# Heads on sixteen even places of each slot, and M0 and N0 made a slot earlier

## The chip, the cores and the metric

The kernel runs on one core of one Trainium2 chip. The metric is the device time in microseconds. A core has five engines that run side by side and are tied together by semaphores: TensorE (PE in the profile; PEld is its loading of weights), VectorE (DVE), ScalarE (ACT), GpSimd (POOL) and SyncE (SP), which here issues all transfers between HBM and the on-chip memory. Products land in PSUM, which has banks of 512 floats per partition.

## The reference

A two-layer encoder does one inference step for 512 prompt frames and eight groups of 16 sample frames: 640 rows of 1024 features. What matters here is branch B of a layer, the gated delta rule with eight heads:

```
h = rmsnorm(x, ln1); proj = h @ w_in                      # all branches at once
q, k, v = silu(causal_conv(qkv)) per head; q, k l2-normed # 128 features a head
for each head:   S_t = a_t (I - b_t k_t k_t^T) S_{t-1} + b_t k_t v_t^T ;  o_t = S_t^T q_t
o = rmsnorm(o, o_norm) * silu(z)
x += (sigmoid(gA) * (zA @ p_a) + sigmoid(gB) * (zB @ p_b)) @ w_o
x += relu(rmsnorm(x, ln2) @ w_up)^2 @ w_down
```

The recurrence is computed in exact block form: a unit lower triangular system over a block of frames is solved, and then a short chain runs over the blocks. Branch A is a gated MLP with a spatial product over 128 frames.

## The kernel before

Activations lie feature by row: 128 partitions of features, 640 rows. A weight block is 128 by 1024; it is loaded by SP (`raw`, three buffers), split by ScalarE and VectorE into a high and a low part (`whi`, `wlo`, lines 133 and 134), and multiplied in three products (high-high, high-low, low-high). One block is 16 units of `gemm` (line 196), a unit being three matmuls of 320 columns.

The order of TensorE's instructions is the program's own: it is scheduled by hand (line 1115). The other engines' orders are worked out when the program is built, from priorities: an instruction counts as so many places earlier as the offset of `tc.high_priority` says. `AHEAD` is 200; the chain below has twice that, the roots 1.

In the phase `heads` of a layer the blocks of q, k, v and of the gates are taken in ten slots of 4, 7, 5, 5, 5, 5, 5, 5, 5 and 6 blocks (line 792). Beside the gemm of slot h three pieces of work for three different heads are laid between its units, each a generator that yields how far ahead its next hop is:

- `prepare` of head h-1: transposes of K (`kt`, line 508) into the two banks of tag "d", squares and the copy `kg` out of them (lines 510 to 512), Gram products (`gp`, three hops) with their masked copies into `AP_` (line 527), transposes of V (`vt`), then the recurrence X on VectorE for the blocks of 16 (lines 577 to 583), the decays E of the next head on ScalarE (line 487), and two hops that join the blocks to 32: `Y3` and `Z3` (lines 601 and 605).
- `chain` of head h-2: makes the masked operands M0 and N0 (lines 624 to 630), joins blocks to 64 and 128 in the hops Y, M1/Z, Y2 and N2, and then runs the chain over four blocks of 128 frames with the hops w, S/o and kS; the sample frames run beside it (`sample`, line 675). Its banks have tag "c", the sample's tag "d".
- `roots` of head h-3: squares of the output, means over 128 features by a product with ones (`ms`, line 767, two halves, tag "d"), a row to HBM (line 777), back as columns, the power -1/2 on GpSimd, and back to HBM (line 784).

Tags "c" and "d" have two banks each, and a product that takes a bank waits until what the bank held has been read. In slot 0 the preparation's place is taken by `gating`: the products for beta and the decay rates, their transposes, a long chain of small VectorE operations (lines 380 to 406), the cumulative sums and a row that goes through HBM. In slot 9 there is no preparation, and the chain of the last head is followed by its roots.

How the hops come to their units is decided in `paced`. Before, each work has a length of its own (`CHAIN` 66, `PREPARE` 70, `ROOTS` 26, `GATING` 48, and the slot's own number of units for roots); a hop that is due at d of length L comes at unit d n / L of n, rounded up. In a slot of five blocks (80 units) that gives these units:

| work | units of its hops |
|---|---|
| chain | 0 (M0, N0), 10 (Y), 15 (M1/Z), 21 (Y2), 26 (N2), 31 (w), 36, 40, 45, 50, 55, 60, 65, 70, 74, 79 |
| prepare | 0 (kt), 13, 18, 22 (gp), 27 (vt), 31, then X from 36 to 68, 76 (Y3), 80 (Z3, behind the slot's last unit) |
| roots | 0, 8 and 18 (ms), 22 |

After the heads, `merge` runs the product for v of branch A (`va`, weights w_v) while `zb` (line 964) loads what the roots left and makes the operand of the next product.

Of the kernel before, what the change touches and what calls it, by code (L numbers as in the profile page):

```python
# [9 lines left out]
F32 = mybir.dt.float32  # L10
# [7 lines left out]
P = 128  # L18
# [4 lines left out]
H = 8  # L23
DEPTH = 2
EPS = 1e-6
NB = 8
# [11 lines left out]

CHAIN, PREPARE, ROOTS, GATING = 66, 70, 26, 48
AHEAD = 200  # L40
# [22 lines left out]
def encoder(ctx, tc, xin, wblk, wba, sct, sdelta, prow, pcol, gates, wst, bsr, convw, consts, delta0,  # L63
# [162 lines left out]

    def paced(work, n, ahead=AHEAD):


        length, gen = work  # L230
        due = 0
        for u in range(n):
            while due * n <= u * length:
                with tc.high_priority(offset=ahead):
                    due += next(gen, length)
            yield
        run(gen)

    def in_turn(first, second):
        yield from first  # L240
        yield 1
        yield from second()
# [116 lines left out]
    def gating(l, pk, pl, out):  # L359
# [4 lines left out]
        if l + 1 < DEPTH:  # L364
            nc.sync.dma_start(wb, wba[l + 1])
        yield 15

# [6 lines left out]
        nc.scalar.activation(v2(baT[0:32, :]), ps[0:32, :, 0:HT], AF.Copy)  # L374
        yield 4
        pt = bank("d", f"baT{l}")
# [30 lines left out]
        gf = g.rearrange("p t h -> p (t h)")  # L407
        yield 24
        pc = bank("d", f"cum{l}")
# [18 lines left out]
        nc.scalar.activation(dec[:, 4:12, :].rearrange("p t h -> p (t h)"), tot[:, 80:144], AF.Exp)  # L428
        yield 6
        pr = bank("d", f"row{l}")  # L430
# [6 lines left out]
        er = later(l, 0, pl, out["gate"])  # L437
        yield 8
        decays(l, 0, pl, out["gate"], er, out)
# [50 lines left out]
    def prepare(l, h, pl, act, gate, out):  # L490
# [24 lines left out]
        nc.vector.scalar_tensor_tensor(sn, sn, -1.0, beta[:, :, h], op0=ALU.mult, op1=ALU.mult)  # L515
        yield 11

        AP_ = pl.tile([P, 5, 2, P], F32, tag="AP", bufs=2, name=f"AP{nm}")
        for ts in ((0, 1), (2, 3), (4,)):
            b = bank("d", f"gp{nm}{ts[0]}")  # L520
            for t in ts:
                o = b[:, (t % 2) * 256:(t % 2) * 256 + 256]
                mm(o[:, 0:P], kT[:, t, :], kT[:, t, :], True, True)
                mm(o[:, P:256], kT[:, t, :], qT[:, t, :], True, True)
            for t in ts:
                o = b[:, (t % 2) * 256:(t % 2) * 256 + 256]
                nc.vector.scalar_tensor_tensor(AP_[:, t], o.rearrange("p (a n) -> p a n", a=2), sn[:, t:t + 1],
                                               rep(E[:, t, :], 1, 2), op0=ALU.mult, op1=ALU.mult)
            if t < 4:
                yield 4  # L530

# [15 lines left out]
        nc.gpsimd.tensor_tensor(qg[:], qT[:], er[:], op=ALU.mult)  # L547
        yield 4
        v0, v1 = tok(vT, f"vt{nm}")
# [3 lines left out]
        nc.vector.tensor_tensor(vn[:, 4:5, :], v1, rep(nk[:, 4:5], 2, P), op=ALU.mult)  # L553
        yield 4
        QT = pl.tile([P, 4, 64], F32, tag="QT", bufs=1, name=f"QT{nm}")
# [6 lines left out]
        if h + 1 < H:  # L562
            er = later(l, h + 1, pl, gate)
        yield 4

# [11 lines left out]
        for j in range(15):  # L577
            n = slice(j + 1, 16)
            nc.vector.tensor_tensor(pr[:, :, n], Bj[j], rep(X[:, :, j], 2, 15 - j), op=ALU.mult)
            if j + 2 < 15:  # L580
                row(j + 2)
            nc.vector.tensor_tensor(X[:, :, n], X[:, :, n], pr[:, :, n], op=ALU.add)
            yield 2
        if h + 1 < H:
# [6 lines left out]
        nc.vector.transpose(m16[:].rearrange("p t n -> p (t n)"), n0c[:, 0:4, :].rearrange("p t n -> p (t n)"))  # L591
        yield 5
        def joined(lhsT, rhs, nm2):
# [9 lines left out]
        nc.scalar.activation(y32[:], by, AF.Copy)  # L603
        yield 4
        bz = joined(y32, n0c, f"Z3{nm}")
        nc.vector.tensor_tensor(n0c[:, 0:4, :], n0c[:, 0:4, :], bz, op=ALU.add)
        sq = pl.tile([P, 5, P], F32, tag="sq", bufs=2, name=f"sq{nm}")
        nc.scalar.activation(sq[:], qT[:], AF.Square, scale=(P * EPS) ** 0.5)
        S8 = pl.tile([P, NB, P], F32, tag="S8", bufs=2, name=f"S8{nm}")
        nc.sync.dma_start(S8[:], sdelta[l, :, h].rearrange("b d e -> d b e"))  # L610
        out[h] = sq, kT, qg, kg, AP_, vn, n0c, QT, S8


    halves = (slice(0, 64), slice(64, 128))
    quarters = tuple(slice(32 * i, 32 * i + 32) for i in range(4))

    def chain(l, h, pl, gate, out):
        sq, kT, qg, kg, AP_, vn, n0c, QT, S8 = out.pop(h)
        beta, ngam, egam, dL, dec, rowd = gate
        kb, qb, N1 = kbs[h % 2], qbs[h % 2], n1s[h % 2]  # L620
        nm = f"{l}{h}"


# [4 lines left out]
        for dst, src, n in ((M0, m0c, 4), (N0, n0c, 5)):  # L628
            for b in range(2):
                nc.vector.tensor_scalar(dst[:, :, 32 * b:32 * b + 32], src[:, 0:n, :], odd[:, b:b + 1], None, op0=ALU.mult)  # L630
        yield 8
        by = bank("c", f"Y{nm}")
# [5 lines left out]
        nc.scalar.activation(Y[:], bys, AF.Copy)  # L638
        yield 4
        b1 = bank("c", f"M1{nm}")  # L640
# [9 lines left out]
        for hf in halves:  # L650
            nc.vector.tensor_tensor(N1[hf, :, hf], bzs[hf], N0[hf, 0:4, :], op=ALU.add)
        yield 5
# [4 lines left out]
        yield 4  # L657
# [4 lines left out]
        yield 4  # L662

# [51 lines left out]
        for t in range(4):  # L715
            if t:
                pk = bank("c", f"kS{nm}{t}")
                mm(pk[:, 0:P], kT[:, t, :], S[:], True, True)
                y = pl.tile([P, P], F32, tag="y", bufs=1, name=f"y{nm}{t}")
                nc.vector.scalar_tensor_tensor(y[:], pk[:, 0:P], egam[:, t, h:h + 1], vn[:, t, :], op0=ALU.mult, op1=ALU.add)  # L720
                if t >= 2:
                    next(beside)
                yield 4
# [5 lines left out]
            yield 4  # L729
# [12 lines left out]
            o_done(po, t)  # L742
            if t < 3:
                yield 4
        nc.sync.dma_start(dp_out[l, h], S[:])
# [3 lines left out]

    def roots(l, h, pl, ond, msd, out):  # L750
        osb, sq = out.pop((h, "o"))
# [19 lines left out]
        nc.sync.dma_start(ond[h], of)  # L771
        yield 8
        means(0, sh)
        sh = squares(1)
        yield 10
        means(1, sh)
        nc.sync.dma_start(msd[0][h:h + 1, :], so[0:1, :])
        yield 4

# [35 lines left out]
    def heads(l, ond, msd, gd, close, norm):  # L815
# [70 lines left out]
        with phase(f"heads{l}", 1) as pl:  # L886
# [15 lines left out]
            for h, slot in enumerate(heads_blocks()):  # L902

                n = 16 * len(slot)
                work = []
                if h == H + 1:
                    work.append(paced((CHAIN + ROOTS, in_turn(
                        chain(l, h - 2, pl, out["gate"], out), lambda: roots(l, h - 2, pl, ond, msd, out))), n, 2 * AHEAD))
                elif h >= 2:
                    work.append(paced((CHAIN, chain(l, h - 2, pl, out["gate"], out)), n, 2 * AHEAD))  # L910
                if h >= 3:
                    work.append(paced((n, roots(l, h - 3, pl, ond, msd, out)), n, 1))
                if 1 <= h <= H:
                    work.append(paced((PREPARE, prepare(l, h - 1, pl, act, out["gate"], out)), n))
                if h == 0:
                    work.append(paced((GATING, gating(l, pl, pl, out)), n))
# [303 lines left out]
```

## Time and profile before

| | |
|---|---|
| median of 3 runs | 2526.88 us (2524.76 to 2527.54) |
| the profiled execution | 2525.81 us, its span 2523.8 us |
| granted TensorE clock | 0.994 |
| busy: TensorE, VectorE, ScalarE, GpSimd | 98%, 52%, 40%, 23% of the span |
| slots 3, 4 and 5 of layer 0, one window each | 52.50, 52.75 and 52.75 us |

The span runs from the first to the last instruction of the profiled execution. A row of a timeline gives start, duration, engine, line, operation, tiles as out<-in, shapes and how often; in brackets stands how long the engine was idle before it and what released it. Matmuls overlap, so the price of one is read from the distance between starts, not from its duration. Products of 32-bit floats appear as two instructions.

### The profile page before, as it was taken

How to read it: one execution, taken by the hardware profiler on the slowest of the kernel's cores; microseconds unless marked ns; L12 is line 12 of the kernel's file. 1: busy time of each engine (PE TensorE's matmuls, PEld its weight loads, DVE VectorE, ACT ScalarE, POOL GpSimd, SP SyncE). 2: the span in 40 equal slices, each digit the busy share in tenths (PEclk: the TensorE clock that was granted, in tenths of full speed). 3: DMA queues.
4: the chain of work that ended last, by engine and by line, in shares of the span. 5: the costliest groups of instructions: out<-in, count | busy, mean ns of one | idle time of the engine just before them, and what ended most of it. 6: DMA issues, size and time to landing. Idle time of an engine off the chain costs nothing. (4 is left out here: it accounts for less than half of the span.)

```text
span 2523.8 us, 45089 instructions
## 1 busy us (share of the span) xinstructions
PE 2466.8 (98%) x18456; PEld 2386.9 (95%) x18456; DVE 1308.1 (52%) x2693; ACT 1020.7 (40%) x1958; POOL 585.5 (23%) x647
## 2 busy tenths in 40 slices
PE   7999999999999999999999999999999999999997
PEld 7999999998999999999999999999989999999997
DVE  7756677536555433333356677664285653333333
ACT  4666666633123212121347666774332222122122
POOL 3223333211222202011213333331112221011012
PEclk9999999999999999999999999999999999999998
DMA  4323323336532222222233333333465222222221
GB/s 153 101 98 114 113 95 95 111 125 240 161 107 68 76 76 76 75 75 74 78 102 110 106 95 95 100 112 114 150 225 150 91 68 76 76 76 76 76 69 65
DMA packets 124237, 261.28 MB, mean 104 GB/s; under 512 B 17232, under 2 KB 56048, under 8 KB 124032
## 3 DMA queue, kind: packets, MB, share of 16 engines
q1 hardware_dynamic: 124032, 258.41, 32.4%
q8 instruction: 145, 2.38, 0.4%
q14 instruction: 60, 0.49, 0.1%
HBM read 218.22 MB, written 40.15 MB: 102 GB/s over the span
## 5 line engine op out<-in xcount | busy, mean ns | idle before, releaser
L133 ACT ACTIVATE whi<-raw 128x1024 fp32r<-128x1024 f32 x304 | 322.1, 1060 | 1027.4 <-issue 352.9
L134 DVE TENSOR_TENSOR wlo<-raw,whi 128x1024 fp32r<-128x1024 f32 x304 | 397.3, 1307 | 160.6 <-ACT whi L133 152.3
L80 PE MATMUL pg_dn<-gl,whi 128*128 128x320 f32 x1024 | 316.6, 309 | 2.1 <-DVE gl L1090 2.1
L80 PE MATMUL pg_up<-Ah,whi 128*128 128x320 f32 x1024 | 317.1, 310 | 0.0
L80 PE MATMUL pg_dn<-gh,whi 128*128 128x320 f32 x1024 | 316.7, 309 | 0.0
L80 PE MATMUL pg_dn<-gh,wlo 128*128 128x320 f32 x1024 | 316.4, 309 | 0.0
L80 PE MATMUL pg_up<-Ah,wlo 128*128 128x320 f32 x1024 | 316.4, 309 | 0.0
L80 PE MATMUL pg_up<-Al,whi 128*128 128x320 f32 x1024 | 316.4, 309 | 0.0
L80 PE MATMUL pg_g<-Ah,whi 128*128 128x320 f32 x896 | 289.6, 323 | 0.0
L80 PE MATMUL pg_g<-Ah,wlo 128*128 128x320 f32 x896 | 276.7, 309 | 0.0
L80 PE MATMUL pg_g<-Al,whi 128*128 128x320 f32 x896 | 276.4, 308 | 0.0
L1089 POOL TENSOR_TENSOR r<-r 128x640 f32<-128x640 f32 x64 | 101.8, 1591 | 684.7 <-ACT gh L1088 684.7
L80 PE MATMUL pg_p<-Ah,whi 128*128 128x320 f32 x768 | 252.2, 328 | 0.0
L80 PE MATMUL pg_p<-Ah,wlo 128*128 128x320 f32 x768 | 237.3, 309 | 0.0
L80 PE MATMUL pg_p<-Al,whi 128*128 128x320 f32 x768 | 236.8, 308 | 0.0
L80 PEld LDWEIGHTS pg_dn<-gl,whi 128*128 128x128 f32 x1024 | 192.3, 188 | 2.6 <-DVE gl L1090 2.6
L80 PEld LDWEIGHTS pg_up<-Ah,whi 128*128 128x128 f32 x1024 | 192.3, 188 | 0.0
L80 PEld LDWEIGHTS pg_up<-Al,whi 128*128 128x128 f32 x1024 | 192.3, 188 | 0.0
L80 PEld LDWEIGHTS pg_dn<-gh,whi 128*128 128x128 f32 x1024 | 192.3, 188 | 0.0
L80 PEld LDWEIGHTS pg_up<-Ah,wlo 128*128 128x128 f32 x1024 | 192.3, 188 | 0.0
L80 PEld LDWEIGHTS pg_dn<-gh,wlo 128*128 128x128 f32 x1024 | 192.2, 188 | 0.0
L80 PEld LDWEIGHTS pg_g<-Ah,whi 128*128 128x128 f32 x896 | 168.6, 188 | 7.6 <-issue 3.5
(688 smaller groups left out, 5414.8 us busy)
## 6 DMA issues: line engine op xcount, KB each, us to landing
raw<-in_wblk SPq DMA_DIRECT2D x304, 512.0 KB, 3.6
gd<-sg SPq DMA_DIRECT2D x56, 320.0 KB, 3.9
rg<-gd SPq DMA_DIRECT2D x48, 320.0 KB, 3.3
S<-in_sdelta SPq DMA_DIRECT2D x16, 512.0 KB, 6.2
out<-S SPq DMA_DIRECT2D x16, 512.0 KB, 3.6
gr<-rowd SPq DMA_DIRECT2D x16, 320.0 KB, 5.3
er<-rowd SPq DMA_DIRECT2D x16, 320.0 KB, 3.9
ond<-osb SPq DMA_DIRECT2D x16, 320.0 KB, 2.2
```

Of the source, the lines that this page charges most:

```text
L80: nc.tensor.matmul(out, lhsT=lhsT, rhs=rhs, start=start, stop=stop, **kw)
L133: nc.scalar.activation(dst_hi, src, AF.Copy)
L134: nc.vector.tensor_tensor(dst_lo, src, dst_hi.bitcast(F32), op=ALU.subtract)
L1089: nc.gpsimd.tensor_tensor(r[:], r[:], r[:], op=ALU.mult)
```

## The change

`paced` loses the lengths. A slot has 16 places (21 in slot 9), evenly spread over its units; at a place each work may do at most one hop, and what a generator yields is now the number of places to its next hop. In a slot of 80 units a place comes every 5 units, and the table becomes:

| work | units of its hops |
|---|---|
| chain | 0 (nothing), 5 (Y), 10 (M1/Z), 15 (Y2), 20 (N2), 25 (w), 30, 35, ... 75 |
| prepare | 0 (kt), 10, 15, 20 (gp), 25 (vt and what was at 31), 30, 35, 40, 45 (X in four parts; decays and n0c with the last), 65 (Y3), 70 (Z3, M0, N0) |
| roots | 0, 15 and 30 (ms), 35 |

At a place the order is chain, roots, preparation. M0 and N0 are made at the end of `prepare` instead of the start of `chain`; the load of the sample states stays behind them. In slot 9 the last head's means come at units 82 and 91 (before 78 and 88), and what follows them behind the last unit, 96 (before 92). In slot 0 the hops of the gating come at 12, 20, 44, 52 and 60 (before 20, 26, 58, 64, 64). The instructions themselves are the same. The core of the diff:

```diff
-CHAIN, PREPARE, ROOTS, GATING = 66, 70, 26, 48
+PLACES, LAST = 16, 21
...
-    def paced(work, n, ahead=AHEAD):
-        length, gen = work
+    def paced(gen, n, places, ahead=AHEAD):
         due = 0
         for u in range(n):
-            while due * n <= u * length:
+            place = -(-u * places // n)
+            if place * n // places == u and place >= due:
                 with tc.high_priority(offset=ahead):
-                    due += next(gen, length)
+                    due = place + next(gen, places)
             yield
         run(gen)
...
# prepare
-        yield 11                      # before the Gram products
+        yield 2
-                yield 4
+                yield 1
-        yield 4                       # between vn and QT
...
-            yield 2                   # every step of X
+            if j in (4, 8, 11):
+                yield 1
...
-        yield 5                       # before Y3
+        yield 4
...
-        yield 4                       # before Z3
+        yield 1
         bz = joined(y32, n0c, f"Z3{nm}")
         nc.vector.tensor_tensor(n0c[:, 0:4, :], n0c[:, 0:4, :], bz, op=ALU.add)
+        m0c = pl.tile([P, 4, 32], F32, tag="m0c", bufs=1, name=f"m0c{nm}")
+        nc.vector.transpose(...)      # m0c, M0, N0: as they stood in chain
+        ...
         sq = ...; S8 = ...
-        out[h] = sq, kT, qg, kg, AP_, vn, n0c, QT, S8
+        out[h] = sq, kT, qg, kg, AP_, vn, M0, N0, QT, S8
...
# chain: every yield of 4 or 5 is 1, its first hop is empty
-        m0c = ...                     # m0c, M0, N0
-        yield 8
+        yield 1
         by = bank("c", f"Y{nm}")
...
# roots(..., gap=3)
-        yield 8
+        yield gap
         means(0, sh)
         sh = squares(1)
-        yield 10
+        yield gap
         means(1, sh)
...
# heads
-                n = 16 * len(slot)
+                n, places = 16 * len(slot), LAST if h == H + 1 else PLACES
...
# gating: yields 15, 4, 24, 6, 8 become 3, 2, 6, 2, 2
```

More of the change, by code (lines that the diff above doesn't have):

```diff
@@ L365, in gating @@
             nc.sync.dma_start(wb, wba[l + 1])
-        yield 15
+        yield 3
         ps = pair(f"ba{l}")
@@ L407, in gating @@
         gf = g.rearrange("p t h -> p (t h)")
-        yield 24
+        yield 6
         pc = bank("d", f"cum{l}")
@@ L428, in gating @@
         nc.scalar.activation(dec[:, 4:12, :].rearrange("p t h -> p (t h)"), tot[:, 80:144], AF.Exp)
-        yield 6
+        yield 2
         pr = bank("d", f"row{l}")
@@ L437, in gating @@
         er = later(l, 0, pl, out["gate"])
-        yield 8
+        yield 2
         decays(l, 0, pl, out["gate"], er, out)
@@ L515, in prepare @@
         nc.vector.scalar_tensor_tensor(sn, sn, -1.0, beta[:, :, h], op0=ALU.mult, op1=ALU.mult)
-        yield 11
+        yield 2
         AP_ = pl.tile([P, 5, 2, P], F32, tag="AP", bufs=2, name=f"AP{nm}")
@@ L553, in prepare @@
         nc.vector.tensor_tensor(vn[:, 4:5, :], v1, rep(nk[:, 4:5], 2, P), op=ALU.mult)
-        yield 4
         QT = pl.tile([P, 4, 64], F32, tag="QT", bufs=1, name=f"QT{nm}")
@@ L603, in prepare @@
         nc.scalar.activation(y32[:], by, AF.Copy)
-        yield 4
+        yield 1
         bz = joined(y32, n0c, f"Z3{nm}")
         nc.vector.tensor_tensor(n0c[:, 0:4, :], n0c[:, 0:4, :], bz, op=ALU.add)
[L607 to L610, printed above, removed]
-        out[h] = sq, kT, qg, kg, AP_, vn, n0c, QT, S8
[L614 to L621, printed above, removed]
         m0c = pl.tile([P, 4, 32], F32, tag="m0c", bufs=1, name=f"m0c{nm}")
@@ L630, in chain @@
                 nc.vector.tensor_scalar(dst[:, :, 32 * b:32 * b + 32], src[:, 0:n, :], odd[:, b:b + 1], None, op0=ALU.mult)
-        yield 8
+        sq = pl.tile([P, 5, P], F32, tag="sq", bufs=2, name=f"sq{nm}")
+        nc.scalar.activation(sq[:], qT[:], AF.Square, scale=(P * EPS) ** 0.5)
+        S8 = pl.tile([P, NB, P], F32, tag="S8", bufs=2, name=f"S8{nm}")
+        nc.sync.dma_start(S8[:], sdelta[l, :, h].rearrange("b d e -> d b e"))
+        out[h] = sq, kT, qg, kg, AP_, vn, M0, N0, QT, S8
+    halves = (slice(0, 64), slice(64, 128))
+    quarters = tuple(slice(32 * i, 32 * i + 32) for i in range(4))
+    def chain(l, h, pl, gate, out):
+        sq, kT, qg, kg, AP_, vn, M0, N0, QT, S8 = out.pop(h)
+        beta, ngam, egam, dL, dec, rowd = gate
+        kb, qb, N1 = kbs[h % 2], qbs[h % 2], n1s[h % 2]
+        nm = f"{l}{h}"
+        yield 1
         by = bank("c", f"Y{nm}")
@@ L638, in chain @@
         nc.scalar.activation(Y[:], bys, AF.Copy)
-        yield 4
+        yield 1
         b1 = bank("c", f"M1{nm}")
@@ L651, in chain @@
             nc.vector.tensor_tensor(N1[hf, :, hf], bzs[hf], N0[hf, 0:4, :], op=ALU.add)
-        yield 5
+        yield 1
         b2 = bank("c", f"Y2{nm}")
@@ L656, in chain @@
         nc.scalar.activation(M1[64:128].rearrange("p t n -> p (t n)"), b2[64:128, 0:256], AF.Copy)
-        yield 4
+        yield 1
         b3 = bank("c", f"N2{nm}")
@@ L661, in chain @@
         nc.vector.tensor_copy(N1[0:64, :, 64:128], b3[0:64, 0:256].rearrange("p (t n) -> p t n", t=4))
-        yield 4
+        yield 1
         osb = pl.tile([P, 5, P], F32, tag="osb", bufs=1, name=f"osb{nm}")
@@ L722, in chain @@
                     next(beside)
-                yield 4
+                yield 1
             pw = bank("c", f"w{nm}{t}")
@@ L728, in chain @@
                 next(beside)
-            yield 4
+            yield 1
             pS = bank("c", f"S{nm}{t}")
@@ L743, in chain @@
             if t < 3:
-                yield 4
+                yield 1
         nc.sync.dma_start(dp_out[l, h], S[:])
@@ L747, in chain, with roots @@
         out[h, "o"] = osb, sq
-    def roots(l, h, pl, ond, msd, out):
+    def roots(l, h, pl, ond, msd, out, gap=3):
         osb, sq = out.pop((h, "o"))
@@ L771, in roots @@
         nc.sync.dma_start(ond[h], of)
-        yield 8
+        yield gap
         means(0, sh)
         sh = squares(1)
-        yield 10
+        yield gap
         means(1, sh)
         nc.sync.dma_start(msd[0][h:h + 1, :], so[0:1, :])
-        yield 4
+        yield 1
         rs = pl.tile([P, 5], F32, tag="rs", bufs=1, name=f"rs{nm}")
@@ L902, in heads @@
             for h, slot in enumerate(heads_blocks()):
-                n = 16 * len(slot)
+                n, places = 16 * len(slot), LAST if h == H + 1 else PLACES
                 work = []
                 if h == H + 1:
-                    work.append(paced((CHAIN + ROOTS, in_turn(
-                        chain(l, h - 2, pl, out["gate"], out), lambda: roots(l, h - 2, pl, ond, msd, out))), n, 2 * AHEAD))
+                    work.append(paced(in_turn(chain(l, h - 2, pl, out["gate"], out),
+                                              lambda: roots(l, h - 2, pl, ond, msd, out, 2)), n, places, 2 * AHEAD))
                 elif h >= 2:
-                    work.append(paced((CHAIN, chain(l, h - 2, pl, out["gate"], out)), n, 2 * AHEAD))
+                    work.append(paced(chain(l, h - 2, pl, out["gate"], out), n, places, 2 * AHEAD))
                 if h >= 3:
-                    work.append(paced((n, roots(l, h - 3, pl, ond, msd, out)), n, 1))
+                    work.append(paced(roots(l, h - 3, pl, ond, msd, out), n, places, 1))
                 if 1 <= h <= H:
-                    work.append(paced((PREPARE, prepare(l, h - 1, pl, act, out["gate"], out)), n))
+                    work.append(paced(prepare(l, h - 1, pl, act, out["gate"], out), n, places))
                 if h == 0:
-                    work.append(paced((GATING, gating(l, pl, pl, out)), n))
+                    work.append(paced(gating(l, pl, pl, out), n, places))
                 for b in slot:
```

1 line of the change is left out of this document (removed).

## The prediction

> **What bounds the kernel.** I read the page's busy table first, then the waits of TensorE, then TensorE and ScalarE in order of time at the start of one head slot.
>
> ```profile
> span 2523.8 us, 45089 instructions
> PE 2466.8 (98%) x18456; PEld 2386.9 (95%) x18456; DVE 1308.1 (52%) x2693; ACT 1020.7 (40%) x1958; POOL 585.5 (23%) x647
> ```
>
> TensorE works for 98% of the span, so time is won only by shortening its program or by taking away its waits. The change leaves the number of products alone, which makes the waits the first place to look:
>
> ```profile
> PE ps_ms L80 <- ACT kg L511: 8.5, 12, 0.7
> ```
>
> It is the only product inside the head slots that the waits name: twelve times, which is slots 3 to 8 of both layers. Here is its place in slot 4 of layer 0, from the slot's start on:
>
> ```profile
> 301.50 0.45 PE L80 MATMUL ps_Z<-n0c,y 32*32 32x32 f32 x32
> 301.90 0.66 PE L504 MATMUL ps_kt04a<-cst,kT 128*128 128x128 f32 x4
> ...
> 302.77 0.31 PE L80 MATMUL pg_p<-Al,whi 128*128 128x320 f32 x1
> ...
> 305.99 0.31 PE L80 MATMUL pg_p<-Ah,wlo 128*128 128x320 f32 x1
> 307.01 0.46 PE L80 MATMUL ps_ms<-sh,onesr 128*1 128x320 f32 x2 [0.71 <-ACT kg L511]
> ...
> 308.04 0.31 PE L80 MATMUL pg_p<-Ah,wlo 128*128 128x320 f32 x1
> 308.27 0.68 PE L80 MATMUL ps_Y<-M,QT 64*64 64x64 f32 x16
> 309.14 0.31 PE L80 MATMUL pg_p<-Al,whi 128*128 128x320 f32 x1
> ```
>
> From 302.77 to 305.99 lie 22 steps of the gemm, so a step is 0.147 us and a unit, three steps, 0.44. The means of the roots (ps_ms) come 8 units after the transposes of K (ps_kt). Both use the bank tag "d", of which there are two, so the means need the first transpose bank back. It is freed by ScalarE's copy kg:
>
> ```profile
> 306.37 0.59 ACT L511 ACTIVATE kg<-ps_kt04a 128x512 f32<-128x512 f32 x1
> 307.10 0.29 ACT L512 ACTIVATE kg<-ps_kt04b 128x128 f32<-128x128 f32 x1
> 309.00 0.39 ACT L638 ACTIVATE Y<-ps_Y 128x256 f32<-128x256 f32 x1 [0.71 <-PE ps_Y L80]
> ```
>
> ScalarE is behind, with a gate's table load and the squares of K ahead of the copy: it ends at 306.96, 4.4 us after the four transposes (301.90 and 0.66), and the means start 0.05 later. Their true price is the distance 305.99 to 307.01 less one step of 0.147: 0.87 us.
>
> **Part 1: the means move from unit 8 to place 3 (unit 15).** At 80 units and 16 places a place is 5 units, 2.2 us of gemm plus the small products at it. The next user of the first K bank is now the first Gram pair at unit 10 (before: 13). From the end of the transposes to it lie 10 units (4.4 us) and the two chain hops Y and M1/Z that stand before it; Y alone is 308.04 to 309.14 less two steps, 0.81 us. So at least 5.2 us, against the 4.4 that ScalarE needs: no wait. The means come two places further and take the second bank, free at 307.39. Gain 12 x 0.87 = 10.4 us; the lower end is 8.5, the idle time alone. Nothing that waits for the means is near: their second half moves from unit 18 to 30, its row to HBM from 22 to 35, and both are read in the merge.
>
> **Part 2: fewer, larger interruptions of the gemm.** A slot now breaks the stream about 22 times (15 chain hops, 2 of the roots, 7 of the preparation, two of them at a shared unit); afterwards 16 times. Is a break itself paid for? A plain one:
>
> ```profile
> 310.16 0.31 PE L80 MATMUL pg_p<-Ah,wlo 128*128 128x320 f32 x1
> 310.31 0.38 PE L80 MATMUL ps_gp<-kT 128*128 128x128 f32 x2
> 310.53 0.39 PE L80 MATMUL ps_gp<-qT,kT 128*128 128x128 f32 x2
> ...
> 311.35 0.31 PE L80 MATMUL pg_p<-Al,whi 128*128 128x320 f32 x1
> ```
>
> From 310.16 to 311.35, less two gemm steps, is 0.90 us for eight matmuls; two of them take 0.22 (310.31 to 310.53), so eight take 0.88. The break is free. A packed hop is not: Y begins 0.23 after the matmul before it (308.04 to 308.27) where the Gram pair begins 0.15 after. The Trainium skill, TensorEngine Tiling (Array Packing), Key Properties, says that changing the tiling mode drains the engine, while another tile of the same mode does not. By that rule only the eight packed hops of a slot pay, and their number is unchanged, so grouping gains nothing; the trace agrees, with the 0.08 us just read, and this keeps the second rival's chance small. What the trace does show is a packed hop with the means right behind it, which the last slot has already:
>
> ```profile
> 522.72 0.31 PE L80 MATMUL pg_g<-Ah,wlo 128*128 128x320 f32 x1
> 522.96 0.67 PE L80 MATMUL ps_Y<-M,AP 64*64 64x64 f32 x8
> 523.56 0.45 PE L80 MATMUL ps_ms<-sh,onesr 128*1 128x320 f32 x2
> 523.86 0.31 PE L80 MATMUL pg_g<-Ah,whi 128*128 128x320 f32 x1
> 524.00 0.31 PE L80 MATMUL pg_g<-Al,whi 128*128 128x320 f32 x1
> ```
>
> Together 522.72 to 524.00 less two steps, 0.99 us. Apart, a packed hop costs 0.81 (Y as stand-in) and the means 0.30 (523.56 to 523.86): 0.12 less together. After the change the first means follow Y2 in slots 3 to 8: 12 x 0.12 = 1.4 us. All other groupings I take at zero; by the same row they could each win or lose up to 0.12 at two places of a slot, 12 x 0.24 = 3 us either way.
>
> **Part 3: M0 and N0 made by the preparation; Z3 to place 14.** One transpose and four scalings leave the first hop of the chain for the end of the preparation, same instructions, same engine. Before, Z3 stands at unit 80, immediately ahead of the next slot's K transposes (301.50, 301.90), and Y follows at unit 10. Afterwards Z3 is at unit 70 and Y at unit 5 of the next slot: 15 units where 10 were, so no wait there. Its own input y32, made at place 13, has 5 units where 4 were. The load of the sample states follows in the same order on SP and is issued earlier; nothing waits for it. Price zero. But Y now ends nearer to ScalarE's backlog (first rival).
>
> **Part 4: the recurrence X, the decays and n0c.** X goes from units 36 to 68 to places 6 to 9 (units 30 to 45), with the decays E of the next head and n0c right behind. In slot 4:
>
> ```profile
> 335.97 1.28 ACT L487 ACT_TABLE_LOAD   x1 [3.04 <-DVE pr L579]
> 340.68 0.25 ACT L668 ACTIVATE w<-ps_w 128x128 f32<-128x128 f32 x1
> 332.70 1.92 POOL L685 TENSOR_TENSOR S<-S,dec 128x1024 f32<-128x1024 f32 x1 [0.22 <-PE ps_qS L80]
> 332.73 1.92 DVE L579 TENSOR_TENSOR pr<-Bs,X 128x20 f32<-128x20 f32 x1
> 340.66 0.38 PE L80 MATMUL ps_w<-y,n 128*128 128x128 f32 x2
> 340.99 0.49 PE L80 MATMUL ps_o<-AP,w 128*128 128x128 f32 x2
> ```
>
> E uses X's workspace and so runs when X is done (about unit 51, well before its place): ScalarE is parked on it for 3.04 us, then loads a table for 1.28, and works through E and what had piled up. What queues behind is the sample's w (340.68), for which TensorE stands 0.11 us late (340.99 instead of 340.88). E now goes earlier, among other hops. I take the balance as zero, from minus 1.3 us (12 x 0.11) to the third rival's price.
>
> **Part 5: the gating of slot 0.** Between its transposes and the cumulative sums lie 24 units instead of 32 (20 and 44 for 26 and 58).
>
> ```profile
> 73.22 0.33 DVE L380 TENSOR_REDUCE gt<-ps_baT 128x80 f32<-128x160 f32 x1 [3.66 <-PE ps_baT L378]
> 84.30 0.23 DVE L406 TENSOR_TENSOR gt<-gt,mis 128x64 f32<-128x64 f32 x1
> ```
>
> The vector chain between them takes 11.3 us (73.22 to 84.53) and would have 24 x 0.44 = 10.6. That chain is stretched by convolutions between its steps and has first claim on DVE, so I expect it to close up: zero, at worst 0.7 us a layer, 1.4.
>
> **Part 6: the last slot and SP.** With 21 places over 96 units the last means come at unit 91, not 88, 1.3 us later; the chain to HBM and back (rs) follows, and SP issues in order.
>
> ```profile
> 570.55 0.32 SPq L784 DMA_DIRECT2D msd<-rs  x1
> 592.96 0.43 SPq L146 DMA_DIRECT2D raw<-in_wblk  x1
> 601.23 0.49 PE L80 MATMUL ps_va<-whi,Ah 128*128 128x512 f32 x1
> 602.62 0.50 PE L80 MATMUL ps_va<-wlo,Ah 128*128 128x512 f32 x1 [0.89 <-DVE wlo L134]
> ```
>
> Behind L784 SP issues the merge's loads one after another; the weight load at 592.96 comes after those of the fourth z tile, which need the first z used up. TensorE already waits for that weight (1.39 us for a step at 601.23). If all of it slides by 1.3 us, each layer loses 1.3; if SP issues other loads while L784 waits, nothing. I take half: plus 1.3 us in all, between 0 and 2.6.
>
> **Sum.** -10.4 - 1.4 + 1.3 = -10.5 us. The profiled execution took 2525.81 us (span 2523.8 and 2.0 around it), giving 2515.3; the median of the runs, 2526.88, is 1.07 above it, so I say 2516.4.
>
> **Rivals.**
> *The wait moves to Y.* Y (unit 5) would end about 3 us after the transposes, in the middle of ScalarE's backlog; if its copy is queued behind the K copies it ends near 307.8, when M1/Z would be due at about 307.2 on the old clock. 0.6 us x 14 slots with a chain ahead of a preparation or roots = 8.4. For it: ScalarE was idle 0.71 us before Y's copy only because Y came late. Against it: the chain's work has the higher priority. Time 2525.
>
> *Every break costs.* If a drain were paid at each, six fewer x 0.12 x 12 slots would add 8.6 us: 2508. Against it stands the free Gram pair.
>
> *ScalarE is parked ahead of a w copy (slower).* E now stands right behind the prompt's second w (place 8), and both need X or TensorE at about the same time. If ScalarE's order puts E ahead of that w while X is late, w waits for the parking of up to 3.04 us and the 1.28 table load. Net of the 2.2 us between hops that is about 2.1 us x 12 slots = 25: 2541. It decides as soon as E's table load starts before that w's product ends. For it: DVE's 20-column product took 1.92 us beside a POOL multiply of 1.92, so X can come late by that much. The Trainium skill, SBUF — State Buffer, Who interferes with whom, says that a DVE instruction with two SBUF inputs and a GpSimd instruction that reads SBUF lock each other out for a whole instruction; the trace agrees, with the two 1.92 us rows. Against it: E follows w in the program and has the lower priority.
>
> *The change does nothing:* the Gram pair inherits the wait for the K bank. It would need ScalarE 0.8 us later than now; 2526.
>
> **How the numbers follow.** Forecast 0.58; wait moves to Y 0.16; every break costs 0.07; parked ScalarE 0.13; nothing 0.06. A difference under 0.2%, 5 us, can't be told from none. Faster is the forecast, the breaks and a third of the Y case: 0.70; the rest of Y, nothing and mild parking: 0.18; slower 0.12. The forecast's own range is -14.8 (10.4 + 1.4 + 3) to -5.9 (8.5 less 2.6), 2512 to 2521. The 80% range takes in the breaks below and the Y case above: 2509 to 2527.
>
> **What would show it.** The waits of TensorE no longer name ps_ms; ps_gp gets none from kg. The slots of five blocks shrink by about 1 us each. Wrong it would be if ps_M, ps_w or ps_S appear there with ACT or DVE as releaser, and the SP part if ps_va's wait stays at 0.89.

## The result, and the profile after

| | before | after |
|---|---|---|
| median of the runs | 2527.21 us (2524.76 to 2528.42) | 2561.57 us (2560.99 to 2562.27) |
| ratio after / before | | 1.0138, 95% interval 1.0125 to 1.015 |
| profiled execution's span | 2523.8 us | 2560.6 us |

The change made the kernel 34.4 us slower; 10.5 us faster was forecast. The head of the page of the kernel after:

```profile
span 2560.6 us, 44967 instructions
PE 2477.7 (97%) x18456; PEld 2395.5 (94%) x18456; DVE 1302.5 (51%) x2693; ACT 1010.1 (39%) x1950; POOL 585.3 (23%) x647
```

TensorE has as many instructions as before and is 10.9 us longer busy on a span 36.8 us longer: it waits more, and some of its work runs slower. From its waits, those that are new or have changed (total, times, longest; `y` from L604 is y32, since numbers in names are left out):

```profile
PE ps_Z L80 <- ACT y L604: 11.4, 12, 1.0
...
PE pg_g L80 <- ACT sg L820: 9.7, 2, 5.0
PE pg_pb L80 <- DVE mix L1017: 8.0, 2, 4.1
PE ps_gp L80 <- ACT kg L511: 5.7, 2, 2.8
...
PE ps_kS L80 <- DVE S L740: 3.5, 12, 0.7
...
PE ps_va L80 <- DVE wlo L134: 1.4, 2, 0.9
```

ps_ms is gone, as forecast. In its place stand two kinds of wait: a few long ones that come once a layer (sg, kg), and short ones that come twelve times (y32, S). Laying both traces side by side by the first product of each slot's first block shows where the time goes:

| stretch | before | after | lost |
|---|---|---|---|
| slot 1, layer 0 | 53.99 us | 66.09 us | 12.1 |
| slots 2 to 9, layer 0 | 421.34 | 427.06 | 5.7 |
| slot 1, layer 1 | 53.80 | 65.02 | 11.2 |
| slots 2 to 9, layer 1 | 421.22 | 427.42 | 6.2 |
| the two merges, to the weights p_a | 251.32 | 253.95 | 2.6 |

Slot 1 loses 23 us of the 37 and is a place that the prediction never looked at. Of the slots behind it, 3 to 7 lose about 1.0 us each and slot 2 loses 1.7; slot 8, in which neither a convolution nor a next head's decays run, is 0.9 us shorter, as forecast for all from 3 to 8.

Slots are counted here from 0, as in the account of the kernel before. The place that the prediction shows as slot 4 has the transposes of head 4 (ps_kt04a) and so is slot 5 by that count, and the three windows that the section on the profile before calls slots 3, 4 and 5 are slots 4, 5 and 6. Nothing in the prediction's sum hangs on it.

### Slot 1: one late copy that grows

ScalarE in slot 1 of layer 0, kernel after (start, duration, in brackets idle before and releaser):

```profile
95.49 1.58 ACT L487 ACTIVATE E<-gr,ngam 128x128 f32<-128x128 f32 x5
...
99.86 0.59 ACT L511 ACTIVATE kg<-ps_kt00a 128x512 f32<-128x512 f32 x1
...
106.54 0.31 ACT L133 ACTIVATE k4p<-kg 128x128 fp32r<-128x128 f32 x1 [5.66 <-POOL kg L543]
...
107.70 0.41 ACT L458 ACTIVATE cb<-pg_p 128x320 f32<-128x320 f32 x1
...
130.18 0.63 ACT L469 ACTIVATE vT<-yb 128x512 f32<-128x512 f32 x1 [3.39 <-DVE yb L467]
...
133.07 1.57 ACT L487 ACTIVATE E<-gr,ngam 128x128 f32<-128x128 f32 x5
...
138.08 0.70 ACT L820 ACTIVATE sg<-pg_g 128x640 f32<-128x640 f32 x1
```

And GpSimd in the same stretch:

```profile
101.50 1.54 POOL L547 TENSOR_TENSOR qg<-qT,er 128x640 f32<-128x640 f32 x1 [7.07 <-DMA er<-rowd]
103.10 0.41 POOL L559 COPY qb<-qg 128x64 f32<-128x64 f32 x2
103.47 1.17 POOL L541 TENSOR_TENSOR dsm<-dsm,phalf 128x5 f32<-128x5 f32 x1
105.25 1.26 POOL L543 TENSOR_TENSOR kg<-kg,dsm 128x640 f32<-128x640 f32 x1 [0.62 <-DVE dsm L542]
```

The decays of head 0 (E at 95.49, with a table load of 1.28 ahead of them) stand in front of the squares of K, so the first bank of K comes free at 100.45: ps_gp waits 2.85 us. The orders of the engines were fixed when the program was built, and in this one GpSimd makes qg ahead of the power that scales kg (103.47). So kg is done at 106.51, and ScalarE, which has a split of kg (k4p) next, stands still for 5.66 us with the convolution's copies (cb) behind it. From there the convolutions run late, the copy vT (130.18) too, behind it the next decays, and last the gate's copy sg at 138.08: TensorE waits 4.7 us for that bank (5.0 in layer 1).

### The clock behind a wait

Windows of the kernel after (length, busy time of PE, PEld, DVE, ACT and POOL, granted clock of TensorE, DMA share and GB/s):

```profile
100.50:102.60 2.10, 2.09 (x9) 2.09 (x10) 0.36 (x2) 0.38 (x3) 1.10 (x1) 0.50 0.03 10
106.00:112.00 6.00, 6.00 (x46) 6.00 (x45) 5.04 (x7) 3.64 (x9) 4.04 (x5) 1.00 0.26 74
...
138.80:144.90 6.10, 6.06 (x23) 6.06 (x24) 1.93 (x1) 0.93 (x1) 2.98 (x4) 0.50 0.42 142
...
1361.60:1364.60 3.00, 2.94 (x22) 2.94 (x23) 0.36 (x2) 0.43 (x4) 2.49 (x4) 1.00 0.03 6
```

Behind both waits of layer 0 TensorE gets half its clock: 6.1 us of steps at 0.50 after the sg wait, which is about 3 us of work lost on top of the 4.7. Behind the same wait for kg in layer 1 (2.85 us again, the last window) it keeps its whole clock. So a wait can cost more than its length in the table of waits, but doesn't always.

### Slots 2 to 7: a step held by GpSimd

Slot 5 of layer 0, kernel after, in order of time:

```profile
346.53 1.91 POOL L687 TENSOR_TENSOR S<-S,dec 128x1024 f32<-128x1024 f32 x1
346.54 2.61 DVE L467 SCALAR_TENSOR_TENSOR yb<-cb,cw,yb 128x664 f32<-128x664 f32 x1
...
349.19 0.91 DVE L467 SCALAR_TENSOR_TENSOR yb<-cb,cw,yb 128x664 f32<-128x664 f32 x1
350.01 0.34 DVE L740 SCALAR_TENSOR_TENSOR S<-S,dec,ps_S 128x128 f32<-128x128 f32 x1
...
350.41 0.49 PE L80 MATMUL ps_kS<-S,kT 128*128 128x128 f32 x2 [0.22 <-DVE S L740]
...
351.55 1.28 ACT L487 ACT_TABLE_LOAD   x1 [0.42 <-DVE pr L578]
...
364.41 0.27 ACT L604 ACTIVATE y<-ps_Y 128x128 f32<-128x128 f32 x1
```

GpSimd's multiplication of the sample states by their decay (S<-S,dec) holds a convolution step: 2.61 us where the next takes 0.91, that is 1.91 and 0.70. Behind it stands another step, then the chain's S, for which TensorE waits (ps_kS). Behind S stand the last steps of X; for the end of X ScalarE is parked with the table load of the next decays (351.55), and y32, for which Z3 waits, is further back in ScalarE's queue (364.41). Before the change the same multiplication held a step of X (the two rows of 1.92 in the prediction), and no product was late for it. In slots 3 to 7 of both layers the kernel after has a convolution step held like this one; in slot 2 it is a step of X (1.88 us), with S, the decays and y32 late all the same. So what counts is what stands behind the held step. The Trainium skill, SBUF — State Buffer, Who interferes with whom, says that a VectorE instruction with two inputs in SBUF contends with a GpSimd instruction that reads SBUF, and calls this contention an exclusive lock; the rows of 1.91 and 2.61 us agree.

### The profile page after: what moved, and what is told of

Read it like the earlier page. It is cut to its first block, busy times and chain, and to the rows that moved or that the text cites. A ratio compares the mean times of both kernels' runs of the same rounds, so it can differ in the third digit from the quotient of the medians.

```text
span 2560.6 us, 44967 instructions
## 1 busy us (share of the span) xinstructions
PE 2477.7 (97%) x18456; PEld 2395.5 (94%) x18456; DVE 1302.5 (51%) x2693; ACT 1010.1 (39%) x1950; POOL 585.3 (23%) x647
## 5 line engine op out<-in xcount | busy, mean ns | idle before, releaser
L134 DVE TENSOR_TENSOR wlo<-raw,whi 128x1024 fp32r<-128x1024 f32 x304 | 404.9, 1332 | 213.2 <-ACT whi L133 198.0
```

Of the source, the lines that this page charges most:

```text
L134: nc.vector.tensor_tensor(dst_lo, src, dst_hi.bitcast(F32), op=ALU.subtract)
```

## The experiments

The runs of each group below share a chip and the runs of the kernel before. Ratios are to the kernel before. From group to group the median of that kernel went from 2526.43 to 2528.04 us, so differences between runs of two groups are uncertain by some 1.6 us.

### Each half of the account alone

**The means alone** (kernel before):

```diff
 # roots, slots 3 to 8
-        yield 8
+        yield 15
         means(0, sh)
         sh = squares(1)
-        yield 10
+        yield 15
         means(1, sh)
         nc.sync.dma_start(msd[0][h:h + 1, :], so[0:1, :])
-        yield 4
+        yield 5
```

> The kernel before, with the roots' two products of ones moved alone: in slots 3 to 8 their hops go from units 8, 18 and 22 to 15, 30 and 35; everything else stays. Theory 1 (the means' part of the change is good and its other parts lose the time): the twelve waits of ps_ms for kg go, 12 x 0.87 = 10.4 us, so about 2517 (2514 to 2519). Rival (the wait is only handed on: the first Gram pair or the vT transposes wait for the same bank, or the means' second half in the middle of the chain costs what was won): 2525 to 2529, with ps_gp or ps_vt in the waits in place of ps_ms.

Measured 2515.26 us, ratio 0.9954 (0.994 to 0.9967): 11.9 us less than before (2527.17). In the head slots the waits name only a gate's product (1.1 us, once) and one ps_kS (0.2 us). Theory 1 holds for the means, and the rival falls.

**The preparation on its old units** (kernel after):

```diff
-paced(prepare(...), n, places)
+spread((70, prepare(...)), n)      # the pacing of before, with its yields
```

> The kernel after, with the preparation alone back on its old units (0, 13, 18, 22, 27, 31, X from 36 to 68 in fifteen steps, Y3 at 76, Z3 at 80); chain, roots and gating stay on the sixteen places, M0 and N0 stay in the preparation. Theory 1 (the earlier places of the preparation put work of ScalarE and VectorE ahead of the copies that TensorE needs): the 5.0 us waits for sg in slot 1 with the slow steps behind them (2 x 7.7) and the waits of Z3 for y32 (11.4 in all) go, and what is left of the loss is slot 1's wait for kg from the gating, so about 2561.6 - 15.4 - 11.4 - 7 = 2528 (2522 to 2534). Rival 1 (the chain's and roots' even places, or the larger groups of hops, cost the time): 2550 or more. Rival 2 (with Z3 at the slot's end and Y five units behind it instead of ten, M0 is late): ps_Y waits for DVE in most slots, some 0.5 to 1 us each, 2535 to 2542.

Measured 2551.86 us, ratio 1.0098 (1.0084 to 1.0112): neither theory 1 nor, in its time, any rival but the first. Other waits took the place of the old ones:

```profile
PE ps_w L80 <- DVE y L732: 9.3, 12, 0.8
...
PE ps_o L80 <- ACT w L680: 4.0, 12, 0.4
PE ps_gp L80 <- ACT kg L521: 3.7, 2, 1.8
...
PE ps_S L80 <- ACT we L717: 2.7, 12, 0.2
```

Half the old layout beside half the new one is a third layout, with a third order on each engine. Such a run can't say which half is to blame, and a later one (below) ran into the same.

**The first decays late** (kernel after, one yield in the gating):

```diff
         er = later(l, 0, pl, out["gate"])
-        yield 2
+        yield 99
```

> The kernel after, with one yield changed: the five exponentials of the first head's decays, which slot 0 issues at place 15, come behind the slot's last unit, as before. Theory 1 (in slot 1 ScalarE does them ahead of the squares of K and so hands the first K bank back 3 us late): the two waits of ps_gp for kg (2.8 us each) and the slower products behind them (about 1.2 each) go, 2561.6 - 8 = 2553 to 2555. Rival (the squares wait for something else as well, or the exponentials then hold up the Gram products' masked copies, which read them): ps_gp's wait stays, or a wait for AP or dg comes in its place, 2559 to 2563.

Measured 2539.56 us, ratio 1.005 (1.0037 to 1.0062): 22.0 us less than after, nearly three times what theory 1 had. Both slot 1s are back at the length of before (53.97 us in both layers), and ps_gp and pg_g have left the waits. ScalarE and GpSimd there:

```profile
96.85 0.59 ACT L511 ACTIVATE kg<-ps_kt00a 128x512 f32<-128x512 f32 x1
...
101.61 0.41 ACT L458 ACTIVATE cb<-pg_p 128x320 f32<-128x320 f32 x1
...
125.94 0.64 ACT L469 ACTIVATE vT<-yb 128x512 f32<-128x512 f32 x1 [1.29 <-DVE yb L467]
...
128.09 0.71 ACT L820 ACTIVATE sg<-pg_g 128x640 f32<-128x640 f32 x1
```

```profile
97.98 1.17 POOL L541 TENSOR_TENSOR dsm<-dsm,phalf 128x5 f32<-128x5 f32 x1 [3.91 <-DVE dsm L513]
99.77 1.26 POOL L543 TENSOR_TENSOR kg<-kg,dsm 128x640 f32<-128x640 f32 x1 [0.62 <-DVE dsm L542]
```

kg is 3.0 us earlier, the power 5.5, cb 6.1, vT 4.2, and the gate's copy is ahead of the next decays, 10.0 us earlier. So the 3 us at the head of slot 1 and the 5 us at its end have one cause, and I had counted them as two.

**The gate's copy first** (kernel after):

```diff
-                gate_act(i, v2(sg[:]), ps[:, :, 0:HT])
+                with tc.high_priority(offset=AHEAD):
+                    gate_act(i, v2(sg[:]), ps[:, :, 0:HT])
```

> The kernel after, with the gates' copies out of PSUM (sg) given the preparation's priority (an offset of 200 at the copy); no hop moves. Theory 1 (in slot 1 ScalarE takes the convolution's end and the five exponentials before the gate's copy, and TensorE stands 5.0 us for that bank and runs at a lower granted clock for some 6 us behind it): the copy goes ahead of the exponentials, the sg waits go, 2 x (5.0 + 2.7) = 15 us less, about 2546 (2543 to 2550). Rival 1 (what is late is the convolution on VectorE, and every order of ScalarE waits for it): sg still waits 3 us or more, 2555 to 2562. Rival 2 (sg ahead of y32 makes Z3 later in the other slots): ps_Z's waits grow above 11.4 us and take back part, 2550 to 2556.

Measured 2550.23 us, ratio 1.0091 (1.0077 to 1.0105), 11.3 us less than after. The wait for sg is gone and the one for kg stays (6.0 us): this mends the end of the sequence alone, and the run before mends its start. It falls short of the 15 us and lies just outside theory 1's range; neither rival's wait shows (ps_Z 11.3 us, as after).

### What is left in slots 2 to 8

**y32 on VectorE** (first decays late):

```diff
-        nc.scalar.activation(y32[:], by, AF.Copy)
+        nc.vector.tensor_copy(y32[:], by)
```

> The kernel after with the first head's decays late (as in the run before this one, 2539.6 us), and the copy y32 between Y3 and Z3 made by VectorE instead of ScalarE. Theory 2 (what is left of the loss, about 1.0 us a slot in slots 2 to 8, is Z3 waiting for y32, which ScalarE does behind a split of a weight and a gate's copy with its table load): the 11.4 us of ps_Z <- y go and with them the 14 x 1.33 us by which the Z3 hops are too long; VectorE is idle there. 2539.6 - 12 to 18: 2522 to 2528. Rival (the larger groups of hops at even places themselves cost the 1.0 us a slot): the wait may go, but the time stays at 2535 or more. Second rival (VectorE's copy is behind a convolution or a split in half the slots): ps_Z then waits for DVE, 2530 to 2536.

Measured 2537.6 us, ratio 1.0038 (1.0024 to 1.0052). ps_Z's wait falls from 11.4 to 2.9 us, but the time by 2: theory 2 falls. The chain was late by then for another reason, and ps_S took up part of it (2.8 us for we).

**Y3 and Z3 two places later** (first decays late):

```diff
-        yield 4                       # before Y3
+        yield 6
```

> The kernel after with the first head's decays late (2539.6 us), and the hops Y3 and Z3 two places later (15 and the slot's end, units 75 and 80, where 76 and 80 were before the change); M0 and N0 then follow at the head of the next slot. Theory 2 (Z3's wait is a matter of where Y3 falls in ScalarE's order, not of the change's second half): ps_Z's 11.4 us go, as y32 then comes behind the gate's copy without waiting for it: 2522 to 2528. Rival 1 (M0 comes too late for Y at place 1, five units behind Z3): ps_Y waits for DVE in most slots, 0.3 to 0.7 us each, 2528 to 2534. Rival 2 (the even places themselves cost 1.0 us a slot): 2535 or more.

Measured 2553.04 us, ratio 1.0101 (1.0087 to 1.0114), 13.5 us more than the run it starts from. That lies in the second rival's range, which has no upper end, but not by its mechanism. Its waits:

```profile
PE ps_S L80 <- ACT we L707: 15.1, 12, 1.3
...
PE ps_w L80 <- ACT whi L133: 5.9, 10, 0.6
```

Y3 is out of the way of ScalarE's backlog, and the sample's copies (we) are in it.

**M0 and N0 in the preparation** (kernel before, the second half of the change alone; the lines as in the diff above, the yields as before):

> The kernel before with the second half of the change alone: M0 and N0 made behind Z3 by the preparation instead of at the head of the chain; every hop stays on its old unit. Theory (as in the prediction: same instructions on the same engine with more room than they need): within 2 us of before, 2525 to 2529, ps_ms still waits 8.5 us for kg. Rival (five VectorE instructions at the slot's end with the lower priority go behind a convolution and make Y late, or hold the squares' readers up at the slot's head): ps_Y waits for M, or ps_ms waits longer, 2530 to 2536.

Measured 2527.91 us, ratio 0.9999 (0.9991 to 1.0008); ps_ms waits its 8.5 us. On the old units this half costs nothing, as the prediction's Part 3 has it.

**Without the sample's decay** (first decays late, y32 on VectorE):

```diff
-            nc.gpsimd.tensor_tensor(S8[:], S8[:], rep(dec[:, 4:12, h], 2, P), op=ALU.mult)
```

> The kernel with the first head's decays late and y32 on VectorE, and GpSimd's multiplication of the sample states by their decay (128x1024, 1.91 us a head) left out: the sample states that come out lack that factor. Theory (ps_kS waits 12 times, 3.5 us, for S, because one step of the convolution on VectorE takes 2.61 us instead of 0.91 while that multiplication runs beside it, and S stands behind it): the wait goes, no convolution step over 1 us at that place, 3 to 6 us less than with it. Rival (S is late because the steps of X are ahead of it in VectorE's order, whatever GpSimd does): the wait stays at 3 us or more and the time within 2 us.

Measured 2516.59 us, ratio 0.9956 (0.9943 to 0.9968): 21.0 us less than with it, where I expected 3 to 6. ps_kS, ps_Z and ps_S are all out of the waits. The 3.5 us of ps_kS were only the part of the damage that a wait named; the delay of X's end went through ScalarE's decays to the copies behind them. This run alone doesn't separate the hold on VectorE from a freer GpSimd. The run with the decay in eight pieces does so in part: GpSimd works longer there, and the time still falls.

### Is it the multiplication, or where it falls?

**The same left out on the old units** (the means moved):

> The kernel before with the means moved (2515.3 us), and GpSimd's multiplication of the sample states by their decay left out (the sample states that come out lack that factor). Theory 3 (that multiplication stops VectorE for 1.9 us in both layouts, but on the old units it falls on a step of X, which nobody is waiting for, and on the even places on a convolution step with the chain's S behind it): without it this kernel gains little, 0 to 4 us, where the even places gained 21: 2511 to 2515. Rival (the multiplication costs the same in every layout, and the 21 us have nothing to do with where the hops lie): 2494 to 2500.

Measured 2513.05 us, ratio 0.9947 (0.9933 to 0.996): 2.2 us less than with it (2515.26), and the two intervals overlap. The same instruction is worth about nothing on the old units and 21 us on the even places. Theory 3 holds.

**The decay in eight pieces** (first decays late):

```diff
+            for b in range(8):
+                nc.gpsimd.tensor_tensor(S8[:, b:b + 1, :], S8[:, b:b + 1, :], rep(dec[:, 4 + b:5 + b, h], 2, P), op=ALU.mult)
```

> The kernel after with the first head's decays late (2539.6 us), and the same multiplication cut into eight of 128x128 on GpSimd, one for each group of sample frames; nothing is left out. Theory 3 (VectorE's convolution step is held for a whole instruction of GpSimd, whatever its length): a step then waits for one piece of about 0.3 us instead of 1.9 and goes between the pieces; S comes 1 us or more earlier, and half or more of the 21 us comes back: 2518 to 2530. Rival (the pieces hold VectorE one after another, because GpSimd gets the next one in ahead of it): the step still takes 2 us or more and the time stays at 2536 to 2545.

Measured 2532.27 us, ratio 1.0021 (1.0013 to 1.003), 7.3 us less, just outside theory 3's range. VectorE in slot 5:

```profile
332.33 1.10 DVE L467 SCALAR_TENSOR_TENSOR yb<-cb,cw,yb 128x664 f32<-128x664 f32 x1
...
333.64 1.10 DVE L467 SCALAR_TENSOR_TENSOR yb<-cb,cw,yb 128x664 f32<-128x664 f32 x1
334.67 0.33 DVE L741 SCALAR_TENSOR_TENSOR S<-S,dec,ps_S 128x128 f32<-128x128 f32 x1
```

A step takes 1.10 us instead of 2.61, and ps_kS is out of the waits: the hold is as long as one instruction of GpSimd (a piece takes 0.39 us when nothing holds it, and 0.39 and 0.70 make 1.09). But ps_Z still waits 11.4 us for y32: the eight pieces run for 4.11 us, other steps are held beside them, and X ends only 0.6 us earlier.

**The decay fused into the update** (first decays late):

```diff
-                nc.vector.tensor_tensor(Sf[...], Sf[...], pS[:], op=ALU.add)
+                for b in range(4 * a, 4 * a + 4):
+                    nc.vector.scalar_tensor_tensor(S8[:, b, :], S8[:, b, :], dec[:, 4 + b, h:h + 1], pS[...], op0=ALU.mult, op1=ALU.add)
```

> The kernel after with the first head's decays late (2539.6 us), and the multiplication gone from GpSimd: the decay is applied in the update of the sample states on VectorE, S = S dec + product, eight instructions of 128x128 in place of two additions of 128x512; nothing is left out. Theory 3: like the run without the multiplication, as VectorE is idle at the end of the chain: 2515 to 2521. Rival (the eight instructions, some 0.35 us each, make the bank or the next hop late on VectorE): 2522 to 2535, with ps_S or ps_kt waiting for S on DVE.

Measured 2518.72 us, ratio 0.9967 (0.9954 to 0.9979), as theory 3 has it. What remains of the waits in the slots:

```profile
PE ps_Z L80 <- ACT y L604: 2.3, 12, 0.3
```

In slots 2 to 7 ScalarE has the same order of instructions in this run, in the one with eight pieces and in the one that both start from. What differs is the time. In slot 5 of layer 0, in us from the slot's first gemm product (at 305.50, 303.53 and 300.55):

| first decays late, and | load for the decays | y32 | end of the slot |
|---|---|---|---|
| nothing else | 33.81 | 46.67 | 53.74 |
| decay in eight pieces | 33.22 | 46.08 | 53.14 |
| decay fused | 32.10 | 44.95 | 52.01 |

The end of X releases that load in all three, y32 follows it by 12.86 us (12.85 in the last), and the slot is shorter by as much as the load is earlier: 0.60 and 1.73 us for 0.59 and 1.71. Over the twelve slots (2 to 7 of both layers) that makes 20.6 us, and the whole program gained 20.8.

The convolution's 144 steps, grouped by line, tell the same of VectorE; before, after, and here (busy time, mean ns | idle before):

```profile
L467 DVE SCALAR_TENSOR_TENSOR yb<-cb,cw,yb 128x664 f32<-128x664 f32 x144 | 137.7, 956 | 26.6 <-ACT yb L465 25.0
```

```profile
L467 DVE SCALAR_TENSOR_TENSOR yb<-cb,cw,yb 128x664 f32<-128x664 f32 x144 | 154.3, 1071 | 14.3 <-ACT yb L465 13.0
```

```profile
L467 DVE SCALAR_TENSOR_TENSOR yb<-cb,cw,yb 128x664 f32<-128x664 f32 x144 | 139.8, 971 | 14.2 <-ACT yb L465 13.1
```

**The same on the old units** (the means moved):

> The kernel before with the means moved (2515.3 us), and the decay applied in the update on VectorE in place of GpSimd's multiplication. If, as theory 3 has it, the multiplication costs the old units only what X loses by it, 2511 to 2516; the best of the kernels so far either way, unless the eight updates on VectorE make a hop late (2517 or more).

Measured 2531.83 us, ratio 1.0014 (1.0005 to 1.0023): a miss, 16.6 us worse than the means alone. In twelve slots the transposes of K wait for the banks that S and Z3's sum (n0c) still hold, for instance

```profile
PE ps_kt04b L504 <- DVE n0c L606: 1.0, 1, 1.0
...
PE ps_kt04a L504 <- DVE S L710: 0.5, 1, 0.5
```

On VectorE four updates take 1.12 us where one addition took 0.69, and a weight's split (wlo, 1.2 us) now comes ahead of n0c. The fusion that wins 21 us in one layout loses 17 in the other.

### Which half of the layout?

**The chain on its old units** (first decays late; `spread((66, chain(...)), n, 2 * AHEAD)` with its yields of before in slots 2 to 8):

> The kernel after with the first head's decays late (2539.6 us), and the chain of slots 2 to 8 back on its old units (0, 10, 15, 21, 26, 31, 36, 40, ... 79); roots and preparation stay on the places, GpSimd's multiplication stays. Theory 3a (the chain's even places bring the multiplication onto the convolution): with them undone it falls on a step of X again, S is not behind it, the waits of ps_kS go and most of the 21 us: 2516 to 2524. Theory 3b (X's earlier places take X out of the multiplication's way, and a convolution step is what is left to hold): the multiplication still holds a convolution step for more than 2 us in slots 3 to 8, and the time stays at 2532 or more. Rival to both (old and new units side by side give waits of their own, as the preparation on old units did): 2545 or more.

Measured 2549.66 us, ratio 1.0085 (1.0072 to 1.0099), the third rival. The multiplication holds a step of X again in most slots (1.81 us in slot 5; in slot 4 it still holds a convolution step, for 2.60), which speaks for 3a, but the convolution and S still stand behind it, and new waits cover what that may have won:

```profile
PE ps_gp L80 <- DVE AP L537: 11.9, 10, 2.4
...
PE pg_g L80 <- ACT cb L470: 6.0, 2, 3.0
```

So 3a and 3b are not told apart.

**The preparation on its old units, first decays late, decay fused:**

> The kernel after with the preparation on its old units and the first head's decays late (the run with the first of these took 2551.9 us), and the decay of the sample states applied in the update on VectorE, so that GpSimd's multiplication is gone. Theory 3 (the waits of ps_w for y, 9.3 us, and of ps_o for w, 4.0 us, come from an X step held 1.86 us by the multiplication with a convolution step and the chain's y behind it): they go, and the time is 2516 to 2526. Rival (X's fifteen steps on their old units are themselves in front of the chain's y): ps_w still waits 5 us or more for y, 2534 to 2545.

Measured 2531.67 us, ratio 1.0018 (1.0009 to 1.0026), 20.2 us less than the run with the preparation alone moved back. ps_w's and ps_o's waits are gone, as theory 3 says, though two edits share the gain; the time stays above its range, and ps_Y now waits 6.3 us for M, the rival named with the first such run.

**Decay fused and y32 on VectorE** (first decays late):

> The kernel after with the first head's decays late and the decay fused into the update (2518.7 us), and y32 copied by VectorE: the last 2.3 us of ps_Z's wait for ScalarE go, 2515 to 2518, level with the means moved alone (2515.3). Rival (as in the run with y32 on VectorE alone, VectorE has it late too, or ScalarE's freed time goes to another order): no gain, 2518 to 2522.

Measured 2517.71 us, ratio 0.9959 (0.9946 to 0.9971). No product of the head slots is left in the waits. This and the means alone (0.9954) both beat the kernel before and the kernel after, and their intervals overlap; the means alone is the smaller edit.

## Why the prediction was wrong

The prediction gave a slower kernel a chance of 0.12 and its slowest rival 2541 us; the kernel took 20 us more than that. By the runs, the 34.4 us are -11.9 (the means) + 22.0 (the first decays) + 20.8 (the held convolution, 2539.56 less 2518.72) + 3.5 that I did not split further; the merges (the wait for mix went from 6.3 to 8.0 us) and the last of ps_Z lie in it. The terms were measured on different kernels, and on the old units the multiplication itself is worth 2.2 us, so this is an account and not an exact sum.

- **Part 1** was right: 10.4 us forecast, 11.9 measured.
- **Part 5** is the step that failed first, priced at zero, at worst 1.4. It followed VectorE's chain to the cumulative sums and stopped there. The decays that moved with it, from behind the slot's last unit to place 15, were not asked what they would stand in front of on ScalarE: the squares of K in slot 1. Cost: 22.0 us.
- **Part 4** failed second, at zero. It took the balance of X, the decays and n0c as nothing; the held step on VectorE made S late, and with X's end the decays on ScalarE and y32 behind them: 20.8 us. The rival of the parked ScalarE came close: the lock, the late X and the parking all happened, and its 25 us are near the 20.8. Its victim was wrong: the prompt's second w is copied ahead of the table load (344.23 against 351.55 in slot 5), and none of the products it named as signs waits. Those that wait are ps_kS and ps_Z. It had a chance of 0.13.
- **Part 3** was right for M0 and N0. Its remark that y32 has 5 units where 4 were did not hold: a split, a table load and a gate's copy came ahead of it on ScalarE, and ps_Z waited 11.4 us. By the last runs that is a consequence of the held step more than a cause: with ScalarE's order the same and the hold gone, y32 comes 1.7 us earlier and 2.3 us of the wait are left.
- **Part 2**: the gain of 1.4 us by grouping is not shown. With no wait left in the slots the even places (decay fused, y32 on VectorE) are level with the old units and moved means: slots 3 to 7 take mostly 51.8 us there and 51.7 here. The rival by which every break costs (8.6 us) falls by the same comparison.
- **Part 6**: ps_va's wait went from 1.8 to 1.4 us, so no loss showed there; of 0 to 2.6, the lower end.
- Of the signs named, ps_ms gone came true. ps_gp did get a wait from kg, in slot 1, where I had asked only about slots 3 to 8, and of the slots of five blocks only slot 8 shrank; 3 to 7 grew by 1.0 us and slot 2 by 1.7.

The common error is in the price "zero" for what moves on engines that are not the bound. I asked whether each result would be ready in time, but not what the moved instructions would stand in front of.

## What to carry to other kernels

When hops move on the engine that bounds, list for every other engine what the moved instructions now stand in front of, and follow that to the next product that needs it, the first slot and the slot borders included. A short lateness can grow where orders are fixed at build time: look for the earliest one, since mending it may remove several waits that look separate. An instruction's price holds for one layout only: leaving one out and measuring, in both layouts, told here what no wait did.

## What the runs showed of the hardware

The clock of TensorE after a wait was not to be told from the wait's length. After 1.84 us idle (the preparation on its old units, first Gram pair of slot 1) the mean over the next 3 us was 0.73:

```profile
101.10:104.10 3.00, 2.98 (x17) 2.98 (x18) 2.11 (x3) 2.15 (x8) 2.94 (x4) 0.73 0.03 6
```

After 3.08 and 3.21 us idle, for mix in the two merges of the kernel before, it was half in one and whole in the other:

```profile
640.30:643.30 3.00, 3.00 (x11) 3.00 (x12) 0.57 (x1) 0.00 (x0) 0.00 (x0) 0.50 0.81 283
...
1883.20:1886.20 3.00, 3.00 (x21) 3.00 (x22) 0.54 (x1) 0.00 (x0) 0.00 (x0) 1.00 1.00 276
```

The Trainium skill, TensorE: Matmul & The Clock Gate, What's actually happening, gives half the clock after at least one idle window of about 3.4 us, by a window that runs freely. The halves agree; that a gap of 1.84 us already led to one does not.
